# Gated delta rule with HGRN2 in one block: two of a chunk's five preparation tiles are allocated in other PSUM banks

## The chip, the cores and the metric

One core of one Trainium2 chip runs the whole program. The metric is device microseconds of one execution; the median of three runs counts. Beside it there is one execution taken by the hardware profiler, and every line of a profile in this document is of such an execution.

## The reference

The reference is one layer of a diffusion backbone. Its input is 2048 latent tokens (a raster, 64 wide) and 256 context tokens, 1024 features each. All tokens go through a layer norm with a modulation and one wide projection `u @ w_in` in float32. Its columns feed two branches of four heads of 128: branch A is a gated delta rule, branch B an HGRN2 recurrence. Both run forwards and backwards, first over the context, then over the latent tokens. The outputs of both branches are normed, gated, projected, merged by sigmoid gates, projected once more and added to the input.

The change lies in branch A. Cut to what matters (a chunk here has 64 tokens, the kernel uses 128):

```python
decay = where(incl, exp(G_i - G_j), 0)              # G: running sum of log a
a_mat = where(strict, (kb @ k.T) * decay, 0)        # kb = k * beta
w, u  = solve(a_mat + I, [kb * exp(G), v * beta])   # unit lower triangular
attn  = (q @ k.T) * decay
# one step of the scan over chunks, S is 128x128 a head
v_new = u - w @ S
o     = (q * exp(G)) @ S + attn @ v_new
S     = S * exp(G_last) + (k * exp(G_last - G)).T @ v_new
```

`q` and `k` have unit norm per token and head, so the sums of their squares are wanted per token.

## The kernel before, in words

The work comes in this order of the source: modulated inputs `u` (split into a high and a low part, `uhi`, `ulo`, so that three matmuls make one float32 product); the projections of branch A with their convolution, written to DRAM as `qkvD` with features on partitions; branch B; then branch A's preparation, solve and levels; the gate projections; branch A's scan; at last the output stage, which reads both branches and the gates from DRAM.

**Preparation (`prep`, lines 761 to 835).** The 2304 tokens are 18 chunks of 128, two of context and sixteen latent. For each chunk `prep` loads `l` (keys, queries, values of four heads, one SBUF buffer, line 766), and makes up to five PSUM tiles of one bank each on TensorE:

- `pt`, shown as `pk` in the profile (line 773): keys transposed to tokens on partitions. ScalarE sums their squares (777) and copies them to `kv` (778).
- `pq` (780, latent chunks only): queries transposed. ScalarE sums their squares (784), and nothing else reads it.
- `pv` (791): values transposed. VectorE scales them into `kv` (794), which is stored to `knvD`.
- `pkk` (812): keys times keys, straight from `l`. VectorE multiplies it with the decay and the step sizes into `an`, eight instructions (817).
- `pkq` (820, latent only): keys times queries, also from `l`. VectorE multiplies it with the decay, two instructions (824), and the result is stored to `atN` (825).

The decay comes from a scan on VectorE (806), an exponential on ScalarE (808) and a mask on GpSimd (810); it depends on none of the five. All five tiles have the tag `t` in the pool `pc`, with `bufs=3`: a slot is given to the next tile when the last reader of its former tile is through.

**Solve and levels (837 to 903).** Groups of four chunks go through `solve` on VectorE (850, 852: 31 elimination steps on 32x32 blocks), then `levels` joins the blocks with small matmuls in `lvt`, one bank. Preparation of one group, levels of the group before and the solve stand in this order in the source (906 to 928).

**Gate projections (`gate_block`, 224 to 233).** 24 blocks of 128 columns, in groups of 512 tokens; a group is 24 matmuls (217 to 219) into a bank of the pool `pj2`, which has two, a copy out on VectorE (232, even groups) or ScalarE (230, odd) and a store to `gT`. Their weights come through one buffer `ws`: load (202), ScalarE (203), GpSimd (204). After the preparation's code stand twenty blocks on token groups 0 and 1 (938 to 939); their groups 2 and 3 are spread over the scan (`late_block`).

**Scan (`stepA`, 959 to 1008).** Eighteen steps, each with one chunk forwards and one backwards. A step's products (`mm4`, 974) go to tiles `psA` in the pool `pd`, two banks with the tag `A`; from step 9 on two in three of them go to four further banks, `pd2`, which are those of `pc`. The scan's SBUF pool takes the place of `u` of groups 0 and 1, so the scan begins once the gate blocks have read these.

The eight PSUM banks while `prep` runs: two of `pj2`, two of `pd`, three of `t`, one of `lv`.

What sets the order: the source is traced once, and a scheduler then orders each engine's instructions at build time, by the order of the source and a simulated timeline (`schedule_with_timeline_sim=True`). It gives out PSUM slots and writes the waits. On the chip each engine and each DMA queue runs its instructions in that fixed order.

Of the kernel before, what the change touches and what calls it, by code (L numbers as in the profile page):

```python
# [8 lines left out]
F32 = mybir.dt.float32  # L9
# [7 lines left out]
P = 128  # L17
# [7 lines left out]
H = 4  # L25
# [14 lines left out]
def block_kernel(ctx, tc, x, c, ctx_in, c_ctx, w_mod, b_mod, w_in, conv_w, a_log, dt_bias,  # L40
# [699 lines left out]
    pd = pdx.enter_context(tc.tile_pool(name="pd", reuse_waits="tile", bufs=2, space=PSUM))  # L740
# [4 lines left out]
    with tc.tile_pool(name="rc", reuse_waits="tile", bufs=2, side="right") as rc, \  # L745
# [15 lines left out]
        def prep(pos):  # L761
# [15 lines left out]
                ac.activation(out=junk, in_=pt[:, h, :], func=AF.Square, accum_out=sk[:, h:h + 1])  # L777
            ac.copy(out=kv[:, 0], in_=pt)
            if lat:
                pq = pc.tile([P, H, P], F32, tag="t", name="pq", bufs=3)  # L780
                for h in range(H):
                    te.transpose(pq[:, h, :], qT[:, h, :], ident)
                for h in range(H):
                    ac.activation(out=junk, in_=pq[:, h, :], func=AF.Square, accum_out=sq[:, ch, h:h + 1])
# [3 lines left out]
            ve.scalar_tensor_tensor(out=nbz[:, :, ch, :], in0=beta[:, :, ch, :], scalar=-1.0,  # L788
                                    in1=sk.unsqueeze(1).to_broadcast([P, 2, H]), op0=ALU.mult, op1=ALU.mult)
            ve.tensor_tensor(out=nbze[:, :, ch, :], in0=nbz[:, :, ch, :], in1=erem[:, :, ch, :], op=ALU.mult)  # L790
            pv = pc.tile([P, H, P], F32, tag="t", name="pv", bufs=3)
            for h in range(H):
                te.transpose(pv[:, h, :], vT[:, h, :], ident)
            ve.tensor_tensor(out=kv[:, 1], in0=pv, in1=nk.unsqueeze(2).to_broadcast([P, H, P]), op=ALU.mult)
# [111 lines left out]
        for i in range(len(grp) + 2):  # L906
            pl = list(range(grp[i][0], sum(grp[i]))) if i < len(grp) else []
            ll = list(range(grp[i - LAG][0], sum(grp[i - LAG]))) if 0 <= i - LAG < len(grp) else []
            if IL == 0:
                for ch in pl:  # L910
                    prep(ch)
                for ch in ll:
                    levels(ch)
            elif IL == 3:
                for ch in ll:
                    levels(ch)
                for ch in pl:
                    prep(ch)
            else:
                while pl or ll:  # L920
                    if pl:
                        prep(pl.pop(0))
                    if ll:
                        levels(ll.pop(0))
                        if IL == 2 and ll:
                            levels(ll.pop(0))
            if 0 <= i - LAG + 1 < len(grp):
                solve(*grp[i - LAG + 1])
# [20 lines left out]
    if True:  # L949
        SA = []  # L950
        for d in range(2):
            t = rd.tile([P, H, P], F32, tag=f"S{d}", name=f"S{d}")
# [291 lines left out]
```

## Time and profile before

| | us |
|---|---|
| median of 3 runs | 2232.41 (2229.06 to 2242.11) |
| the profiled execution | 2233.26 |
| its span, first to last instruction | 2231.6 |
| busy: TensorE, weight loads, VectorE, ScalarE, GpSimd | 2114.9, 1767.6, 1404.9, 925.3, 688.2 |
| mean granted TensorE clock | 0.985 of full speed |

PE is TensorE, PEld its weight loads, DVE VectorE, ACT ScalarE, POOL GpSimd, SPq the queue of DMAs. Matmuls overlap in the pipeline, so the duration of one (388 ns at 512 columns) is longer than its share of the engine's time. A wait is listed as "engine line waited for: us in total, times, longest"; a line of a timeline gives start, duration, engine, line, tiles, number of instructions and in brackets the idle time before it with what ended it.

### The profile page before, as it was taken

The page shows a single profiled execution, that of the slowest core. Times are in us where ns is not written, and L with a number is a line of the kernel's source. Part 1 is how long each engine was busy: PE and PEld are TensorE (multiplying, and loading weights), DVE is VectorE, ACT ScalarE, POOL GpSimd, SP SyncE. Part 2 cuts the span into 40 slices and gives each one's busy share as a digit, 9 for nine tenths or more (in the row PEclk, how much of TensorE's full clock was granted, in tenths as well). Part 3 has the DMA queues.
Part 4 walks back from the last instruction along what each step waited for, and adds up shares of the span by engine and source line. Part 5 has one row for each costly group of instructions (what it writes and reads, how often), then busy time and mean ns, then how long its engine had stood idle before and what let it go on. Part 6 is the DMA issues. An engine that isn't in the chain of part 4 may idle for free. (4 is left out here: it accounts for less than half of the span.)

```text
span 2231.6 us, 40198 instructions
## 1 busy us (share of the span) xinstructions
PE 2114.9 (95%) x15056; PEld 1767.6 (79%) x15056; DVE 1404.9 (63%) x3225; ACT 925.3 (41%) x2334; POOL 688.2 (31%) x672
## 2 busy tenths in 40 slices
PE   8999999999999999999998988999989888999998
PEld 3778888888888888888776776788778877888887
DVE  4826666727776777786588788733332348766665
ACT  4623222224443444443455554344453354444441
POOL 3413433412222323234333332221133224433331
PEclk9999999999999999999999999999999999999999
DMA  9312222223323433336777778776888864444432
GB/s 340 110 35 76 64 71 77 83 76 95 106 87 100 126 95 104 101 104 195 219 224 225 255 241 214 228 231 208 236 276 278 258 228 147 145 136 127 142 95 80
DMA packets 308277, 348.15 MB, mean 156 GB/s; under 512 B 78635, under 2 KB 218161, under 8 KB 308083
## 3 DMA queue, kind: packets, MB, share of 16 engines
q1 hardware_dynamic: 306067, 338.26, 49.1%
q0 software_dynamic: 2016, 7.34, 0.9%
q8 instruction: 118, 1.93, 0.4%
q14 instruction: 76, 0.62, 0.1%
HBM read 230.46 MB, written 115.06 MB: 155 GB/s over the span
## 5 line engine op out<-in xcount | busy, mean ns | idle before, releaser
L217 PE MATMUL ps<-uhi,wh 128*128 128x512 f32 (+1 forms) x1824 | 708.2, 388 | 2.9 <-DVE uhi L306 2.6
L218 PE MATMUL ps<-ulo,wh 128*128 128x512 f32 (+1 forms) x1824 | 707.6, 388 | 3.4 <-POOL ulo L311 1.7
L219 PE MATMUL ps<-uhi,wl 128*128 128x512 f32 (+1 forms) x1824 | 705.3, 387 | 0.0
L218 PEld LDWEIGHTS ps<-ulo,wh 128*128 128x128 f32 x1824 | 345.9, 190 | 66.7 <-POOL ulo L311 2.8
L217 PEld LDWEIGHTS ps<-uhi,wh 128*128 128x128 f32 x1824 | 345.7, 190 | 66.4 <-DVE uhi L306 3.9
L219 PEld LDWEIGHTS ps<-uhi,wl 128*128 128x128 f32 x1824 | 345.6, 189 | 62.1 <-POOL wl L204 0.4
L204 POOL TENSOR_TENSOR wl<-ws,wh 128x512 fp32r<-128x512 f32 x144 | 200.2, 1391 | 551.7 <-ACT wh L203 494.4
L203 ACT CAST wh<-ws 128x512 fp32r<-128x512 f32 x144 | 89.4, 621 | 309.5 <-DMA ws<-in_w_in_dram 213.9
L419 DVE SCALAR_TENSOR_TENSOR acc<-raw,cols,acc 128x512 f32<-128x512 f32 x192 | 152.8, 848 | 0.9
L1143 PE MATMUL py<-yh,wab 128*128 128x256 f32 x512 | 145.9, 286 | 5.8 <-DVE mg L1146 5.4
L1144 PE MATMUL py<-yl,wab 128*128 128x256 f32 x512 | 145.1, 284 | 1.3 <-POOL yl L1126 1.3
L1145 PE MATMUL py<-yh,wab 128*128 128x256 f32 x512 | 144.6, 283 | 0.0
L1162 PE MATMUL pso<-uhi,mh 128*128 128x512 f32 x256 | 102.6, 402 | 7.8 <-ACT mh L1148 4.7
L605 POOL TENSOR_TENSOR bg<-s,fz 128x512 f32<-128x512 f32 (+1 forms) x36 | 37.8, 1049 | 224.9 <-ACT X L585 86.7
L1143 PEld LDWEIGHTS py<-yh,wab 128*128 128x128 f32 x512 | 97.7, 191 | 8.0 <-DVE mg L1146 6.6
L1164 PE MATMUL pso<-uhi,ml 128*128 128x512 f32 x256 | 102.2, 399 | 0.6 <-DVE ml L1149 0.6
L1163 PE MATMUL pso<-ulo,mh 128*128 128x512 f32 x256 | 101.8, 398 | 0.0
L1144 PEld LDWEIGHTS py<-yl,wab 128*128 128x128 f32 x512 | 97.7, 191 | 2.1 <-POOL yl L1126 1.7
L1145 PEld LDWEIGHTS py<-yh,wab 128*128 128x128 f32 x512 | 98.7, 193 | 0.2
L1126 POOL TENSOR_TENSOR yl<-gt,yh 128x512 fp32r<-128x512 f32 x32 | 45.0, 1408 | 148.3 <-ACT yh L1125 148.3
L998 DVE SCALAR_TENSOR_TENSOR S<-S,gl,psA 128x128 f32<-128x128 f32 x136 | 38.3, 342 | 82.5 <-PE psA L979 82.4
L1136 ACT ACTIVATE mg<-mg 128x512 f32<-128x512 f32 x64 | 40.4, 632 | 113.0 <-DMA mg<-gT 110.4
(374 smaller groups left out, 3942.3 us busy)
## 6 DMA issues: line engine op xcount, KB each, us to landing
ws<-in_w_in_dram SPq DMA_DIRECT2D x144, 256.0 KB, 3.4
gT<-gt SPq DMA_DIRECT2D x96, 256.0 KB, 3.6
kv<-knvD SPq DMA_DIRECT2D x36, 512.0 KB, 5.1
kq<-qkvD SPq DMA_DIRECT2D x32, 512.0 KB, 6.0
an<-atN SPq DMA_DIRECT2D x32, 512.0 KB, 6.2
mg<-gT SPq DMA_DIRECT2D x64, 256.0 KB, 3.4
qkvD<-acc SPq DMA_DIRECT2D x48, 256.0 KB, 2.3
l<-qkvD SPq DMA_DIRECT2D x16, 768.0 KB, 6.5
```

Of the source, the lines that this page charges most:

```text
L203: ac.copy(out=wh[:, j:j + 4, :], in_=ws)
L204: po.tensor_tensor(out=wl[:, j:j + 4, :], in0=ws, in1=wh[:, j:j + 4, :].bitcast(F32), op=ALU.subtract)
L217: te.matmul(out=ps, lhsT=wh[:, k, :], rhs=uhi[gi][:, k, :], start=(k == 0), stop=False)
L218: te.matmul(out=ps, lhsT=wh[:, k, :], rhs=ulo[gi][:, k, :], start=False, stop=False)
L219: te.matmul(out=ps, lhsT=wl[:, k, :], rhs=uhi[gi][:, k, :], start=False, stop=(k == KB - 1))
L419: ve.scalar_tensor_tensor(out=a_, in0=raw[:, o + k:o + k + n], scalar=wk, in1=a_, op0=ALU.mult, op1=ALU.add)
L1143: te.matmul(out=py[:, i, :], lhsT=wh[:, k, ms_], rhs=yh[i][:, k, :], start=(k == 0), stop=False)
L1144: te.matmul(out=py[:, i, :], lhsT=wh[:, k, ms_], rhs=yl[i][:, k, :], start=False, stop=False)
L1145: te.matmul(out=py[:, i, :], lhsT=wl[:, k, ms_], rhs=yh[i][:, k, :], start=False, stop=(k == H - 1))
L1162: te.matmul(out=ps, lhsT=mh[:, k, ts_], rhs=wout[0][k][:, ns], start=(k == 0), stop=False)
L1163: te.matmul(out=ps, lhsT=mh[:, k, ts_], rhs=wout[1][k][:, ns], start=False, stop=False)
L1164: te.matmul(out=ps, lhsT=ml[:, k, ts_], rhs=wout[0][k][:, ns], start=False, stop=(k == KB - 1))
```

## The change

`pq` and `pv` are allocated in the pool `pd` with the tag `A` (two banks, the scan's `psA`) instead of `pc` with the tag `t`. `pk`, `pkk` and `pkq` stay in the three slots of `t`.

```diff
--- before.py
+++ after.py
@@ -777,7 +777,7 @@
                 ac.activation(out=junk, in_=pt[:, h, :], func=AF.Square, accum_out=sk[:, h:h + 1])
             ac.copy(out=kv[:, 0], in_=pt)
             if lat:
-                pq = pc.tile([P, H, P], F32, tag="t", name="pq", bufs=3)
+                pq = pd.tile([P, H, P], F32, tag="A", name="pq")
                 for h in range(H):
                     te.transpose(pq[:, h, :], qT[:, h, :], ident)
                 for h in range(H):
@@ -788,7 +788,7 @@
             ve.scalar_tensor_tensor(out=nbz[:, :, ch, :], in0=beta[:, :, ch, :], scalar=-1.0,
                                     in1=sk.unsqueeze(1).to_broadcast([P, 2, H]), op0=ALU.mult, op1=ALU.mult)
             ve.tensor_tensor(out=nbze[:, :, ch, :], in0=nbz[:, :, ch, :], in1=erem[:, :, ch, :], op=ALU.mult)
-            pv = pc.tile([P, H, P], F32, tag="t", name="pv", bufs=3)
+            pv = pd.tile([P, H, P], F32, tag="A", name="pv")
             for h in range(H):
                 te.transpose(pv[:, h, :], vT[:, h, :], ident)
             ve.tensor_tensor(out=kv[:, 1], in0=pv, in1=nk.unsqueeze(2).to_broadcast([P, H, P]), op=ALU.mult)
```

## The prediction

> **What bounds the kernel now.** I read the head of the page first (busy time of each engine), then the engines' busy time in four stretches: before the delta rule's preparation, the preparation, the scan, the output stage.
>
> ```profile
> PE 2114.9 (95%) x15056; PEld 1767.6 (79%) x15056; DVE 1404.9 (63%) x3225; ACT 925.3 (41%) x2334; POOL 688.2 (31%) x672
> ```
>
> Columns of the next view: stretch, its length, busy time and instruction count of PE, PEld, DVE, ACT, POOL, granted clock, DMA share, GB/s.
>
> ```profile
> 0.00:1036.00 1036.00, 1011.89 (x6905) 821.35 (x6906) 693.07 (x1563) 392.05 (x686) 330.35 (x332) 0.99 0.34 105
> 1036.00:1364.00 328.00, 294.86 (x2107) 241.00 (x2106) 257.89 (x676) 172.52 (x586) 113.99 (x130) 0.98 0.77 236
> 1364.00:1800.00 436.00, 403.30 (x3528) 346.50 (x3528) 179.61 (x538) 185.93 (x589) 100.47 (x114) 0.98 0.78 240
> 1800.00:2232.00 432.00, 404.80 (x2521) 358.77 (x2519) 274.32 (x451) 174.84 (x473) 143.44 (x97) 0.98 0.42 133
> ```
>
> TensorE is the bound of the whole; another engine matters only where it makes TensorE wait. In the preparation (second row, 328 us) TensorE is busy 294.86 us and idle 33.1 us; DVE, with 257.89 us, comes next. What the 33.1 us wait for is in the list of TensorE's waits over the same stretch (waiter, releaser, total us, times, longest):
>
> ```profile
> PE pkk L814 <- ACT kv L778: 9.2, 9, 1.5
> PE pkq L822 <- ACT junk L784: 8.0, 9, 2.8
> PE pkq L822 <- DVE kv L794: 6.1, 5, 1.7
> PE pk L775 <- DMA l<-qkvD: 5.5, 4, 1.9
> ...
> PE pv L793 <- DVE dec L824: 0.5, 1, 0.5
> ```
>
> The first three rows are what the change touches. `pkk` and `pkq` multiply tiles that already lie in SBUF (`kT`, `qT`), so the squares and copies named as releasers (L778, L784, L794) give them no data; they free a PSUM slot. Five tiles of a chunk share a ring of three: `pkk` gets the slot of `pk`, and `pkq` that of `pq` or `pv`. The three rows add up to 23.3 us. One chunk in the timeline (start, duration) shows why the slot is late:
>
> ```profile
> 1115.14 0.60 PE L775 MATMUL pk<-ident,l 128*128 128x128 f32 x4
> ...
> 1119.20 0.63 ACT L808 ACTIVATE dec<-dec 128x512 f32<-128x512 f32 x1 [2.75 <-DVE dec L806]
> ...
> 1121.16 0.26 ACT L777 ACTIVATE junk<-pk 128x128 bf16<-128x128 f32 x1
> ...
> 1123.24 1.16 PE L814 MATMUL pkk<-l 128*128 128x128 f32 x8 [0.91 <-ACT kv L778]
> ...
> 1124.71 1.16 PE L822 MATMUL pkq<-l 128*128 128x128 f32 x8 [0.31 <-ACT junk L784]
> ...
> 1127.04 0.52 SPq L766 DMA_DIRECT2D l<-qkvD  x1
> ```
>
> `pk` is in PSUM at about 1115.7, but ACT squares it only at 1121.16, behind the exponential of the decay (L808), which had itself waited for DVE. TensorE fills the 8.1 us between `pk` and `pkk` with gate matmuls, comes to `pkk` before ACT is through, and stands. The next load of `l` goes out only at 1127.04, after `pkq`, the last reader of its single buffer.
>
> The waits also cost clock. The granted clock is the third number from the end in these rows; the row after them is the `pkq` inside the first one:
>
> ```profile
> 1220.00:1230.00 10.00, 7.14 (x34) 5.92 (x36) 9.62 (x36) 6.39 (x24) 3.69 (x6) 0.83 0.69 182
> 1260.00:1270.00 10.00, 9.34 (x71) 7.70 (x72) 8.58 (x30) 6.34 (x22) 2.28 (x2) 0.83 0.89 316
> 1300.00:1310.00 10.00, 8.23 (x44) 6.63 (x45) 9.48 (x31) 5.29 (x20) 3.64 (x3) 0.66 0.69 233
> ```
>
> ```profile
> 1224.01 2.08 PE L822 MATMUL pkq<-l 128*128 128x128 f32 x8 [1.88 <-ACT junk L784]
> ```
>
> The eight `pkq` matmuls took 2.08 us there, against 1.16 us in the chunk above. Of 10 us each, 0.17 + 0.17 + 0.34 of full speed is missing: 6.8 us of work.
>
> **The change, part by part.** No instruction, DMA or byte is added or removed. The 16 `pq` and 18 `pv` tiles (four transposes each) go to two other banks; nothing moves past another instruction in the source. The banks are the scan's:
>
> ```profile
> L979 PE MATMUL psA<-S,kq x544: 270/275/426, 1362.4 to 1793.7; 128*128 128x128 f32 x182
> ```
>
> Its first matmul starts at 1362.4, when the preparation is over, so the two banks lie idle until then and their new tenants delay nothing. If the last chunk's `pv` holds a bank when the scan is ready, the scan loses at most its DVE read, under 1 us. I take 0.
>
> *Removed.* With `pk`, `pkk` and `pkq` alone in a ring of three, no tile waits for another of its own chunk: 23.3 us go, and the 0.5 us of `pv` behind L824 too; 23.8 us.
>
> *Added.* The next chunk's `pkk` and `pkq` now take slots that this chunk's DVE reads free (L817, L824). All five groups can follow each other at once, so the reload of `l` can go out some 9 us earlier, and TensorE can run up to a chunk ahead until it meets those reads. The order on each queue is fixed when the kernel is built, from modelled durations; where the chain of preparation runs later on the chip than in that plan, TensorE stands at the next slot. That it does run late shows in a wait of DVE's:
>
> ```profile
> DVE dec L806 <- DMA atN<-dec: 22.6, 10, 5.7
> ```
>
> The decay tile waits for its own store, 22.6 us in ten scans; that stays. Bounds of the new wait: 0.5 us (the `pv` row, the only one in which a tile waits for the previous chunk's DVE read) and 23.8 us (the same lateness, met at another slot). I take 9.2 us, the `pkk` row, as the nearest: about one wait of 1 us in every second of the 18 chunks, at the first of the two tiles that meet the limit, the second then following it. Behind a waiting `pkk` stand `pkq` and the gate matmuls, so it is lost in full, as now. Less than 0.5 us is excluded unless other waits shrink too (the rival on the chain); more than 23.8 us takes another mechanism (the rival on DVE). `pk` waiting for `l`, 5.5 us, may fall with the earlier issue or rise with a closer plan: 0 to twice that, so I leave it as it is.
>
> *Clock.* Of these waits 14.6 of 23.8 us go; in proportion the clock gives 6.8 x 14.6 / 23.8 = 4.2 us, between 0 and 6.8.
>
> The Trainium skill ("TensorE: Matmul & The Clock Gate", section "HAM oscillation — how this bites in real kernels") warns of idle gaps above about 3.4 us as what drops the clock. The trace differs: a stretch with clock 0.83 follows a wait of 1.88 us. By the rule the clock term would be 0 and the sum 4.2 us less.
>
> *Does the gain reach the end?* While the scan runs, gate matmuls share its queue. The scan's matmuls (first fence) and the gate's (second) in the same two stretches:
>
> ```profile
> 1700.00:1725.00 25.00, 9.57 (x80) 1.00 0.84 264
> 1775.00:1800.00 25.00, 18.89 (x149) 0.96 0.82 275
> ```
>
> ```profile
> 1700.00:1725.00 25.00, 17.05 (x72) 1.00 0.84 264
> 1775.00:1800.00 25.00, 2.09 (x9) 0.96 0.82 275
> ```
>
> Beside 72 gate matmuls in 25 us the scan gets 80 of its own through; beside 9 it gets 149. So fill slows the scan, not its own chain alone, and fill done earlier lets the scan end earlier. The output stage follows. I carry the gain over in full; the least is 0 (first rival).
>
> *Sum.* 14.6 + 4.2 = 18.8 us off. The profiled execution took 2233.26 us (span 2231.6, 1.7 around it): 2233.3 - 18.8 = 2214.5. The median of the runs is 0.85 us lower, so 2214 us.
>
> **Rivals.**
>
> *The waits only move (no change).* 18 chunks in 328 us are 18.2 us each, on a chain of decay scan, exponential, squares, products and store. If that chain is about 1.3 us a chunk longer than planned, TensorE loses it at some slot, L817's if not L778's; then the 23.8 us come back, and the clock with them: 2233 less a few us, about 2230. For it: the store waits, untouched and as large as the sum. Against it: a chunk's squares can now run ahead of the exponential that held them up, which shortens the chain. That the scan's banks are not free would end here too; the 1362.4 speaks against it.
>
> The Trainium skill (same page and section) tells of a matmul kernel in which double-buffering PSUM gave no further gain. It speaks for this rival; here three rows of waits name the slot, so I leave its chance as the rows give it.
>
> *DVE takes over (slower).* Chunks packed closer put their DVE work in a row ahead of the gate's copies (L232), which free the projection's two banks.
>
> ```profile
> L806 DVE TENSOR_TENSOR_SCAN dec<-gb,after 128x512 f32<-128x512 f32 x36 | 47.6, 1324 | 37.9 <-DMA atN<-dec 22.6 <-issue 9.4 <-DMA gb<-gD 5.1
> ...
> L817 DVE SCALAR_TENSOR_TENSOR an<-pkk,nbz,dec 128x128 f32<-128x128 f32 x137 | 37.8, 342 | 0.2
> L824 DVE TENSOR_TENSOR dec<-pkq,dec 128x512 f32<-128x512 f32 x30 | 20.6, 686 | 1.8 <-PE pkq L822 1.4
> ...
> L232 DVE COPY gt<-ps 128x512 f32<-128x512 f32 x19 | 13.0, 682 | 0.6 <-PE ps L219 0.5
> ```
>
> ```profile
> PEld ps L217 <- DVE gt L232: 0.3, 1, 0.3
> ```
>
> A chunk's burst is 2 x 1.32 + 8 x 0.342 + 2 x 0.686 = 6.8 us. A group of 24 gate matmuls takes 24 x 17.05 / 72 = 5.7 us, so a copy (0.68 us) may be 5.0 us late before TensorE stands. Behind a whole burst each of 19 copies costs 1.8 us, 34 us: 2214.5 + 34 = about 2248. It decides from 18.8 / 19 = 1 us a copy, a lateness of 6 us. For it: DVE's 257.89 of 328 us. Against it: 0.3 us of such waits now, and copies spread through the burst.
>
> *The chain itself gets shorter (more gain).* With squares and products early, all of the 33.1 us and 6.8 us of clock could go: 2233.3 - 39.9 = 2193.
>
> **How the numbers follow.** The forecast has 0.48: 2214, its own range 2203 (new waits 0.5 us, clock in full) to 2222. No change 0.29, about 2230; slower, about 2248, 0.14; more gain, about 2193, 0.09. From these: faster 0.57, same 0.29, slower 0.14, with 0.5% of 2232, 11 us, as what a measurement of this kernel can tell. The range takes in the no-change case with some us above and nearly all of the larger gain: 2195 to 2238; the slower rival is left out.
>
> **What the profile afterwards would show.** Right: TensorE's waits of `pkk` and `pkq` on L778, L784, L794 gone; the five groups of a chunk in one run; fewer stretches below clock 1.00 between 1036 and 1364; the scan's first matmul some 19 us before 1362.4; the scan's first bank with no wait on L794. Wrong: waits of `pkk` or `pkq` on L817 or L824 near 20 us (first rival), waits of the gate's matmuls on L232 (DVE), or a scan that starts earlier and ends at 1793 as now, the freed time then idle in the third stretch.

## The result: slower by one per cent, and the profile after

The changed kernel takes 2257.57 us (median of 6 runs, 2253.49 to 2261.01), the kernel before, run beside it, 2235.89 us (6 runs): a ratio of 1.0101 [1.0082, 1.0120]. The profiled execution took 2258.08 us, its span is 2256.4 us, 24.8 us more than before.

First the head of the page of the changed kernel:

```profile
PE 2123.3 (94%) x15056; PEld 1774.9 (79%) x15056; DVE 1411.1 (63%) x3225; ACT 926.5 (41%) x2334; POOL 683.8 (30%) x672
```

TensorE runs the same 15056 matmuls. It is idle for 2256.4 - 2123.3 = 133.1 us, against 2231.6 - 2114.9 = 116.7 us before: 16.4 us. The other 8.4 us are busy time, for the same work at a lower clock: 0.980 against 0.985. Now the stretches, cut at the scan's first and last matmul (columns as in the prediction):

```profile
0.00:1036.00 1036.00, 1011.71 (x6902) 820.69 (x6903) 691.44 (x1562) 392.47 (x686) 324.85 (x332) 0.99 0.34 105
1036.00:1382.70 346.70, 301.01 (x2082) 246.36 (x2080) 286.19 (x730) 177.37 (x596) 114.14 (x131) 0.96 0.75 225
1382.70:1822.40 439.70, 404.74 (x3546) 348.50 (x3547) 157.98 (x482) 181.61 (x579) 100.42 (x114) 0.96 0.76 236
1822.40:2256.40 434.00, 405.82 (x2530) 359.36 (x2529) 275.50 (x452) 175.03 (x476) 144.38 (x98) 0.98 0.42 134
```

The same two middle stretches of the kernel before, with the scan's own cuts:

```profile
1036.00:1362.40 326.40, 293.26 (x2067) 239.56 (x2066) 256.33 (x673) 172.52 (x586) 113.27 (x130) 0.98 0.77 236
1362.40:1797.90 435.50, 402.80 (x3560) 346.19 (x3559) 181.13 (x541) 185.19 (x587) 101.18 (x115) 0.98 0.78 240
```

The stretch before the scan is 20.3 us longer, the scan 4.2 us, the rest is unchanged. Before the scan TensorE is idle for 346.70 - 301.01 = 45.7 us, against 33.1: 12.6 us. And (1 - clock) times the length is about 13.9 us, against 6.5: 7.4 us (the clock here has two digits; stretches of 10 us give 13.7 and 6.8). The two give 20.0 of the 20.3 us.

Yet the preparation itself became faster. Key transposes (`pk`, L775), first of the kernel before, then of the changed one (count, duration min/median/max, first and last start):

```profile
L775 PE MATMUL pk<-ident,l x72: 270/272/330, 1038.6 to 1352.6; 128*128 128x128 f32 x72
```

```profile
L775 PE MATMUL pk<-ident,l x72: 270/273/447, 1039.2 to 1294.6; 128*128 128x128 f32 x72
```

The last chunk's keys are transposed 58 us earlier. What TensorE waits for instead, between 1030 and 1400 us of the changed kernel:

```profile
PE pk L775 <- DMA l<-qkvD: 17.7, 9, 3.6
PE ps L217 <- DVE gt L232: 6.8, 4, 3.3
PE lvt L888 <- DVE N L885: 4.5, 4, 3.1
PE pkq L822 <- DVE dec L824: 4.3, 5, 1.4
PE psA L979 <- POOL wl L204: 2.9, 1, 2.9
PE lvt L900 <- DVE yt L897: 2.5, 2, 2.1
PE lvt L876 <- ACT Nb L902: 1.9, 1, 1.9
```

No row names L778, L784 or L794 any more: the 23.8 us are gone. Taken by tile, up to the scan's first matmul, these waits replace them (before in brackets): `pk` 19.0 (5.5), the levels' `lvt` 11.4 (3.7), the gates' `ps` 7.9 (0), `pkq` 4.3, the scan's first `psA` 2.9 (0). That is 13.5 + 7.7 + 7.9 + 4.3 + 2.9 = 36.3 us more for 23.8 us less, 12.5 us net, which is the idle time found above.

The timeline of one chunk of the changed kernel shows where the largest comes from:

```profile
1101.91 0.63 PE L775 MATMUL pk<-ident,l 128*128 128x128 f32 x4 [0.72 <-DMA l<-qkvD]
...
1103.24 1.06 PE L814 MATMUL pkk<-l 128*128 128x128 f32 x8
...
1104.14 1.06 PE L822 MATMUL pkq<-l 128*128 128x128 f32 x8
...
1105.29 1.22 DVE L806 TENSOR_TENSOR_SCAN dec<-gb,after 128x512 f32<-128x512 f32 x1
1106.54 2.79 SPq L802 DMA_DIRECT2D gb<-gD  x2
...
1109.42 0.38 SPq L766 DMA_DIRECT2D l<-qkvD  x1
...
1115.23 0.63 PE L775 MATMUL pk<-ident,l 128*128 128x128 f32 x4 [2.09 <-DMA l<-qkvD]
```

The five groups follow each other without a gap. `l` is free when `pkq` ends at 1105.20. But its reload goes out at 1109.42, because the two loads of the gate rows (`gb`, L802) stand ahead of it in SP's queue, and they wait for the decay scan on VectorE that reads their buffers (L806). `l` lands about 5.8 us after its issue, and TensorE stands for 2.09 us. Of the 15 reloads that follow a `pkq`, the middle one goes out 4.2 us after it in the changed kernel and 1.2 us before the change. And with some 18 us a chunk, a delay was then mostly hidden: 5.5 us of waits in all.

### The profile page after: what moved, and what is told of

Its sections match the earlier page's. It is cut to its first block, busy times and chain, and to the rows that moved or that the text cites. A ratio compares the mean times of both kernels' runs of the same rounds, so it can differ in the third digit from the quotient of the medians.

```text
span 2256.4 us, 40213 instructions
## 1 busy us (share of the span) xinstructions
PE 2123.3 (94%) x15056; PEld 1774.9 (79%) x15056; DVE 1411.1 (63%) x3225; ACT 926.5 (41%) x2334; POOL 683.8 (30%) x672
## 5 line engine op out<-in xcount | busy, mean ns | idle before, releaser
L422 POOL TENSOR_TENSOR acc<-acc,sg 128x512 f32<-128x512 f32 (+1 forms) x56 | 71.6, 1296 | 47.8 <-ACT sg L421 47.8
```

## The experiments

Two theories were tested. *Queue:* with packed chunks the reload of `l`, late in SP's queue, takes the place of the ring, and the gates' copies behind VectorE (L232) add to it. *Levels:* VectorE does more of the preparation early, its first solve comes later, and the levels and the scan with it. A third reason stood beside both: an edit can make the scheduler order thousands of instructions anew, and the new order may be worse by itself. In the recorded expectations this third reason is called scatter; packing is the general form of *Queue*, conservation says that TensorE makes up the same lateness at some other wait, and the waits theory is that TensorE's waits set the time, not the start of the levels. Ratios are to the kernel before, run beside each.

### The two tiles one at a time

```diff
 # e2_pq_only, e18_pq_again: pq in pd, pv as before
-            pv = pd.tile([P, H, P], F32, tag="A", name="pv")
+            pv = pc.tile([P, H, P], F32, tag="t", name="pv", bufs=3)
 # e3_pv_only: pv in pd, pq as before
-                pq = pd.tile([P, H, P], F32, tag="A", name="pq")
+                pq = pc.tile([P, H, P], F32, tag="t", name="pq", bufs=3)
```

> Only pq goes to the scan's banks; pv stays in the ring with pk, pkk and pkq. One tile per chunk (pkq) then still waits for a slot of its own chunk (pk, freed by ACT L778). Packing theory: period between 13.5 and 18 us, time between before and after, ratio 1.000 to 1.010. Conservation theory: about 1.000 to 1.005, the waits at pkq on L778. Scatter theory: no order between this run, the next and the full change.

> Only pv goes to the scan's banks; pq stays in the ring. As with pq alone, pkq waits for pk's slot. Packing theory: as with pq alone, ratio 1.000 to 1.010, period the same within 1 us. Conservation theory: 1.000 to 1.005. Scatter theory: may lie over 0.7% away from pq alone.

> The kernel before with `pq` alone in the scan's banks, the same kernel as in e2_pq_only, timed in five rounds to narrow its ratio. If that version is truly faster: ratio 0.994 to 0.998, waits of `pkq` on `kv` near 11 us again, since the order is fixed when the kernel is built. Rival (its 0.4% was the chip's day): ratio 0.998 to 1.002.

`pq` alone: 0.9959 [0.9940, 0.9977], and in the second series 2225.88 us, 0.9974 [0.9957, 0.9991]. `pv` alone: 0.9978 [0.9964, 0.9992]. Each half is faster than the kernel before, the whole is slower. Neither packing nor conservation had this: both put the halves at 1.000 or above. TensorE's waits of `pq` alone (second series) before the scan:

```profile
PE pkq L822 <- ACT kv L778: 9.8, 9, 2.2
PE ps L217 <- ACT gt L230: 5.7, 1, 5.7
PE pk L775 <- DMA l<-qkvD: 5.4, 4, 2.8
```

Four tiles in three slots keep a ring wait of about 10 us, and `l` stays at its old 5.4 us. The stretch before the scan is still 9.9 us longer than before (336.3 us); the gain of 19.7 us lies in the scan (415.8 us):

```profile
1036.00:1372.30 336.30, 298.83 (x2145) 244.24 (x2144) 277.88 (x731) 175.54 (x595) 106.99 (x125) 0.95 0.77 234
1372.30:1788.10 415.80, 393.84 (x3464) 338.35 (x3463) 160.41 (x480) 181.61 (x576) 103.12 (x116) 0.99 0.78 246
```

VectorE has 160 us of work left in the scan instead of 181, and TensorE is idle there for 22.0 us instead of 32.7. That less VectorE work makes the scan shorter is not shown: the changed kernel has only 158 us of it left there, and its scan is the longer one. So neither stretch may be read alone; their sum counts: 761.9 us before, 752.1 here, 786.4 in the changed kernel.

### The reload of the keys, queries and values

Three edits of the changed kernel aim at `l`: hold each load of `l` until the previous chunk's `kv` has been stored (slower pace); put the loads of `gb` on GpSimd's queue; or split `l` into three tiles with a load each.

```diff
 # e1_pace
+            with tc.issue_after(kvs[0]) if kvs[0] is not None else ExitStack():
...
-            sy.dma_start(out=knvD[ch], in_=kv)
+            kvs[0] = sy.dma_start(out=knvD[ch], in_=kv).ins
 # e9_gb_pool
-                sy.dma_start(out=gb, in_=gD[d, ch].rearrange("h t -> (h t)").partition_broadcast(P))
+                po.dma_start(out=gb, in_=gD[d, ch].rearrange("h t -> (h t)").partition_broadcast(P))
 # e10_l_split
+            lt = [rc.tile([P, H, P], F32, tag=f"l{j}", name=f"l{j}", bufs=1) for j in range(3)]
+            for j in ((0, 1, 2) if lat else (0, 2)):
+                sy.dma_start(out=lt[j], in_=qkvD[ch, :, j])
```

> The changed kernel, with the load of the next chunk's l put behind the store of this chunk's kv in the SP queue, about where it went out before the change. Two banks as changed. Packing theory (the chunks follow each other too closely: TensorE then stands at the reload of l, 17.7 us, behind gate copies, 9.2 us, and at the levels, 11.3 us): the period goes back to about 18 us, the ring's waits stay away, so faster than before by up to 1% (ratio 0.990 to 1.000). Conservation theory (TensorE makes up the preparation chain's lateness at whichever slot or buffer comes next): about 24 us of waits come back at pk on l, ratio 1.000 to 1.005. Scatter theory (any new order of instructions moves the time by a per cent): ratio anywhere from 0.99 to 1.015, with waits in other places.

> The changed kernel, with the loads of gb (the decay's input) issued by GpSimd's queue instead of SP's. In the changed kernel the reload of l goes out 4 to 6 us after pkq, its last reader, because two gb loads that wait for VectorE stand ahead of it in SP's queue (before: 0.3 to 3 us); TensorE then waits 17.7 us for l. Queue theory: l goes out within 2 us, the waits of pk on l fall below 8 us, and the time falls by 10 us or more against the changed kernel, ratio to before 1.000 to 1.006. Landing theory (the loads land later than planned because the DMA engines are busier): waits of pk on l stay at 15 us or more. Scatter theory: time does not follow the waits on l.

> The changed kernel with l as three tiles and three loads of 256 KB (keys, queries, values), each freed by its own last reader; the order in SP's queue is the planner's. pk needs only the keys, which land in about 3.5 us instead of 6.9. Both queue and landing theory: waits of pk on l below 8 us, time down by about 10 us against the changed kernel, ratio to before 1.000 to 1.006. If the waits at the gate's copies and the levels count for as much, the time stays above 1.006.

Measured: 1.0011 [0.9992, 1.0029], 1.0003 [0.9986, 1.0020] and 1.0030 [1.0015, 1.0045]; `pk` waits 11.4, 7.3 and 9.9 us in all. Each gives back 0.7 to 1.0 of the 1.0%. The split stays above its expected 8 us; its loads of 256 KB land after 4.4 us (median), not 3.5. With `gb` on GpSimd's queue TensorE waits before the scan for:

```profile
PE ps L217 <- DVE gt L232: 9.3, 3, 3.1
PE pk L775 <- DMA l<-qkvD: 7.3, 6, 3.1
PE pkq L822 <- DVE dec L824: 5.5, 7, 2.0
PE pkk L814 <- DVE an L817: 5.5, 4, 1.7
```

The wait on `l` falls from 17.7 to 7.3 us, those on the gates' copies and on the ring's DVE reads rise: idle time before the scan goes from 45.7 to 38.7 us only. The Trainium skill ("DMA: Bandwidth & Descriptors", section "Issuing engines are not separate DMA queues") says that issuing from several engines only saves the issuing time, usually small beside the transfer. Here it was not the issue itself that took time: in the chunk above the `l` load stood 4 us behind a load that waited. With `gb` elsewhere the middle reload goes out 1.2 us after `pkq`.

If the queue matters only for packed chunks, the same edit must give nothing elsewhere. It was made in the kernel before and in the one with `pq` alone:

> The kernel before with the one line of the gate rows' load (`gb`, L802) on GpSimd's queue; none of the two tiles moved. Theory (the loads of `gb` hold up the reload of `l` only where the preparation is packed as in the kernel after): before, `pk` waits for `l` only 5.5 us and the ring of three waits 23.8 us, so the edit finds little to give back; ratio 0.997 to 1.003, ring waits 18 to 26 us, `pk` 3 to 7 us. Rival (moving `gb` is worth about 1% in any kernel, and the change has no part in it): ratio 0.988 to 0.993. Second rival (any edit that replans moves the time by up to 0.5% either way): outside 0.997 to 1.003 with no wait that accounts for it.

> Only pq in the scan's banks, gb loads on GpSimd's queue. Queue theory: little to win, since pk waits only 4 us for l there: ratio 0.993 to 0.997, as pq alone within its interval. Scatter theory: may lie 0.7% away from pq alone.

In the kernel before it costs 0.4%: 1.0039 [1.0022, 1.0056]; there `pk` waits for `l` 3.6 us and the ring waits, with `pv`, are 17.7 us. With `pq` alone: 1.0044 [1.0026, 1.0062], against 0.9959 and 0.9974 without the edit, so 0.7 to 0.9% worse. Only the fully changed kernel gains, by 1.0%. So the edit has no general merit. But both controls lie outside what the queue theory had expected (0.997 to 1.003 and 0.993 to 0.997), where the third reason had put them, so they do not show that the changed kernel gained by the queue and not by a new order. In the control no single wait accounts for the loss: TensorE is idle for 110.2 us in all, 6.5 us less than before, and its clock is 0.981 against 0.985. Its profiled execution, 2235.16 us, is also the fastest of its ten (median 2242.01), so the trace shows little of the 0.4%.

### The gates' copies

```diff
 # e11_gate_copies_act; e13_gb_pool_copies_act has the gb edit as well
-            if g % 2:
+            if g % 2 or (g == 0 and i >= 24 - NLATE):
                 ac.copy(out=as_rows(t), in_=col_to_row(ps))
```

> The changed kernel, with the copies of group 0 of the twenty late gate blocks on ScalarE (all of their copies before the scan then are). DVE theory: the waits of the gate's matmuls on L232 (6.8 us) go and VectorE is freed of about 14 us in the stretch, so the levels' waits on VectorE (7 us of 11.4) shrink: down by 8 to 15 us against the changed kernel, ratio to before 1.003 to 1.007. If ScalarE is as late as VectorE, the waits turn up on L230 and the ratio stays at 1.010.

> The changed kernel with gb loads on GpSimd's queue and the gate's early copies on ScalarE, two edits which alone gave 1.000 and 1.002 where the change alone gave 1.010. If the losses are sums of waits: gains add, ratio 0.990 to 0.995. If the order chosen decides (scatter): ratio 0.997 to 1.006, no better than one of them.

With the late blocks' copies of group 0 on ScalarE: 1.0021 [1.0008, 1.0034]; the waits of `ps` fall from 7.9 to 3.9 us, but `pk`, too, from 19.0 to 12.3, and `lvt` rises to 16.9. Both edits together: 1.0010 [0.9993, 1.0027], no better than the `gb` edit alone, with `lvt` at 21.4 us. The repairs don't add: what one wait gives up, the next takes.

### The first solve and the start of the levels

Two edits move the first solve forward: VectorE may not start the second group's preparation before `fin`, the last step of the first solve (`e5`), or the first group has two chunks instead of four (`e6` the changed kernel, `e7` the kernel before, `e8` `pq` alone).

```diff
 # e5_hold
+                with tc.issue_after(fin) if i == 1 else ExitStack():
                     for ch in pl:
                         prep(ch)
 # e6, e7, e8
-        grp = [(c0, min(CG, NC - c0)) for c0 in range(0, NC, CG)]
+        grp = [(0, NC % CG)] + [(c0, CG) for c0 in range(NC % CG, NC, CG)]
```

> The changed kernel, with VectorE's instructions of the second group's preparation (chunks 4 to 7) queued behind the last step of the first solve. Levels theory: the first solve takes 79 us in the changed kernel (51 before) because the closer packed preparation comes between its steps on VectorE; so levels start later and the chain solve, levels, scan ends later. Freed of that, the first solve takes about 30 us, the first level's store comes near 1175 instead of 1214, and the end moves by most of it: 2220 to 2235 us, ratio to the changed kernel 0.985. Waits theory (TensorE's 45.7 us idle before the scan set the time): the preparation is held up, TensorE waits as much or more, 2250 us or above.

> The changed kernel with groups of 2, 4, 4, 4, 4 chunks instead of 4, 4, 4, 4, 2; the same five solves, the same work. Levels theory: the first solve can begin after two chunks, near 1065 instead of 1089; the first level's store comes 30 to 60 us earlier than 1214 and the end 20 to 45 us earlier: 2212 to 2237 us. Waits theory: no change beyond 0.5%, 2247 to 2268 us.

> The kernel before the change with groups of 2, 4, 4, 4, 4. Levels theory: the first level's store 30 to 50 us ahead of 1198, the end 15 to 40 us earlier, ratio 0.982 to 0.993. Waits theory: ratio 1.000 within 0.4%, since no wait of the ring goes.

> Only pq in the scan's banks, groups of 2, 4, 4, 4, 4. Levels theory: both gains add, ratio to before 0.978 to 0.990, the fastest of all. Waits theory: as pq alone, 0.996.

1.0063 [1.0048, 1.0078], 1.0045 [1.0028, 1.0063], 1.0088 [1.0073, 1.0103] and 1.0093 [1.0077, 1.0110]. `e5` and `e6`, 2245.4 and 2242.7 us, fall between what the levels theory and the waits theory expected; `e7` and `e8` miss both. The levels' first matmuls (L876; count, durations, first and last start) in the kernel before and in `e7`:

```profile
L876 PE MATMUL lvt<-n,an x576: 185/191/213, 1163.5 to 1619.0; 32*32 32x32 f32 x192
```

```profile
L876 PE MATMUL lvt<-n,an x576: 184/191/238, 1129.4 to 1619.7; 32*32 32x32 f32 x192
```

The levels start 34 us earlier, end 0.7 us later, and the kernel is slower. In the changed kernel they start 42 us (`e5`) and 27 us (`e6`) earlier, and the gain is 0.4 and 0.6%, no more than other edits of it give. So an earlier start of the levels does not explain the time by itself, and the levels theory fell. Nor does the wait on `l`: it is longer in `e6` than in the changed kernel,

```profile
PE pk L775 <- DMA l<-qkvD: 21.5, 11, 4.1
```

and about the same in `e5`, 21.4 us, and yet both are faster than the changed kernel.

### The order itself

Four edits that change no dependence, only where a tile's matmuls stand in the source: `pv`'s transposes ahead of the small VectorE operations, or `pkk` ahead of the decay, in both kernels.

```diff
 # e4_pv_early (before), e14_after_pv_early
+            pv = pd.tile([P, H, P], F32, tag="A", name="pv")      # e4: pc, tag "t", bufs=3
+            for h in range(H):
+                te.transpose(pv[:, h, :], vT[:, h, :], ident)
             ve.tensor_scalar(out=sk, in0=sk, scalar1=EPS, scalar2=None, op0=ALU.add)
 # e16_before_pkk_early, e15_after_pkk_early: pkk and its four matmuls right behind the store of kv
```

> The kernel before the change, with pv's allocation and transposes written in the source ahead of the five small instructions on the squares (L785 to L790). No resource changes. Packing and conservation theories: ratio 1.000, within 0.3%, waits of pkk and pkq in the ring about 23 us as before. Scatter theory: the time moves by 0.5% or more.

> The changed kernel with pv's allocation and transposes ahead of the five small instructions in the source, the neutral edit that left the kernel before at 0.9995. Waits theory: ratio to before 1.008 to 1.012, as the change. Scatter theory: 1.000 to 1.006 is as likely, with the scan's stretch back at 422 to 427 us from 439.7.

> The changed kernel with pkk's allocation and its four matmuls ahead of the decay in the source; they depend on l alone, so no resource changes. Waits theory: 1.008 to 1.012. Scatter theory: anywhere from 0.998 to 1.012.

> The kernel before the change with the same move of pkk. Waits theory: 1.000 within 0.3%, the ring's waits at about 23 us. Scatter theory: 0.993 to 1.010.

Before: 0.9995 [0.9981, 1.0010] and 0.9990 [0.9974, 1.0006]. Changed: 1.0110 [1.0073, 1.0147] and 1.0104 [1.0069, 1.0138], with `pk` at 18.0 and 21.1 us. The one per cent stands against these edits. They are hardly a test, though: in the traces at most 27 of the 15056 places in TensorE's order of matmuls hold another matmul, while the change itself alters 4403 of them and the `gb` edit 3839. So they show that this one order loses 1.0% each time, not that another order of the changed source would.

### Kernels side by side

Idle and clock loss ((1 - clock) times span) are TensorE's, of the one profiled execution; the ratio is that of the timed runs.

| kernel | ratio | span | idle | clock loss | span less both |
|---|---|---|---|---|---|
| before | 1 | 2231.6 | 116.7 | 33.5 | 2081.4 |
| changed | 1.0101 | 2256.4 | 133.1 | 45.1 | 2078.2 |
| e2, `pq` alone | 0.9959 | 2217.0 | 109.8 | 28.8 | 2078.4 |
| e18, the same | 0.9974 | 2222.7 | 113.5 | 28.9 | 2080.3 |
| e3, `pv` alone | 0.9978 | 2227.5 | 114.6 | 35.6 | 2077.3 |
| e9, changed + `gb` queue | 1.0003 | 2230.7 | 112.5 | 37.9 | 2080.3 |
| e13, e9 + copies | 1.0010 | 2232.7 | 114.7 | 40.2 | 2077.8 |
| e11, changed + copies | 1.0021 | 2236.6 | 119.5 | 33.5 | 2083.6 |
| e10, changed + `l` split | 1.0030 | 2241.5 | 121.0 | 40.3 | 2080.2 |
| e17, before + `gb` queue | 1.0039 | 2233.4 | 110.2 | 42.4 | 2080.8 |
| e7, before + small first group | 1.0088 | 2247.4 | 125.7 | 36.0 | 2085.7 |
| e15, changed + `pkk` early | 1.0104 | 2258.5 | 126.1 | 51.9 | 2080.5 |

TensorE's own work is 2077 to 2086 us in all of these, and 2072 to 2079 us in the eight kernels that the table leaves out; what differs is the time that it stands and the clock that it loses.

## Why the prediction was wrong, step by step

- **TensorE is the bound.** Right, as the last column shows.
- **Removed, 23.8 us.** Right: the three rows are gone, the five groups run in one piece, and the preparation ends 58 us earlier. The store wait of `dec`, which was to stay at 22.6 us, fell to 5.2 us.
- **Added, 9.2 us at L817 and L824, and `pk` "as it is".** This is the step that failed. The new slot waits were small (4.3 us, all on L824), but the other ends of the same chain were not priced. The waits of `pk` went from 5.5 to 19.0 us, 17.7 of them on `l`, outside their bounds of 0 to 11; the gates' `ps` waits 7.9 us instead of none and the levels' `lvt` 11.4 instead of 3.7. With the `psA` wait, 36.3 us were added where 9.2 were priced. The text saw that "the reload of `l` can go out some 9 us earlier" and looked neither at what stands ahead of it in SP's queue nor at the 5.8 us that it takes to land. `e9` shows the queue's part in the wait: with `gb` out of the way `pk` waits 7.3 us. What that part is worth in time is not shown (below).
- **DVE takes over (rival).** Right in kind, too high in size: 6.8 us of waits on L232, not 34.
- **The levels (no term).** `lvt` rose by 7.7 us, and 7.9 of its 11.4 us are waits on VectorE (2.3 of 3.7 before). That they stand behind VectorE's preparation work, which now falls closer together, is a reading, not tested.
- **Clock, 4.2 us gained.** Wrong in sign. Shorter ring waits did not bring clock; the new waits are longer and cost more. By 10-us stretches between 1036 and the scan, the loss went from 6.8 to 13.7 us.
- **Does the gain reach the end.** Not tested as meant, since the scan started 20 us later. In `pq` alone it went the other way round: the scan started 10 us later, and ended 10 us earlier.
- **The sum.** 23.8 us out and 36.3 us in before the scan, 7.4 us of clock on top, 4.2 us in the scan: 24.1 of the 24.8 us, where 18.8 us of gain were forecast. The rival "the waits only move" had the right mechanism, but put it at one slot and let it give back no more than it took.

What stays open. In the scan the changed kernel waits in more places than the one with the `gb` edit. First the changed kernel's largest waits there, then those of `e9`:

```profile
PE psA L979 <- ACT vx L985: 13.1, 10, 4.7
PE psA L979 <- DVE r L991: 7.3, 5, 2.2
PE psA L979 <- ACT o L985: 4.7, 2, 2.7
PE psA L979 <- DMA an<-atN: 2.9, 2, 2.1
```

```profile
PE psA L979 <- ACT vx L985: 5.3, 7, 1.1
PE psA L979 <- DMA an<-atN: 4.4, 4, 3.5
PE psA L979 <- ACT o L985: 3.4, 3, 2.0
PE psA L979 <- DVE r L991: 1.3, 1, 1.3
```

No `l` is loaded in the scan and its source is the same, so the order that the scheduler chose is the likely reason for these 12.5 us of idle time (35.0 against 22.5). The two stretches of `e9`:

```profile
1036.00:1373.70 337.70, 299.04 (x2073) 242.07 (x2071) 292.17 (x730) 174.81 (x592) 129.65 (x163) 0.97 0.77 230
1373.70:1798.10 424.40, 401.88 (x3553) 345.21 (x3553) 160.60 (x483) 184.12 (x582) 101.91 (x115) 0.97 0.78 245
```

Of the 25.7 us by which its span is shorter than the changed kernel's, 9.0 lie before the scan and 15.3 in it. The other edits agree: the scan takes 439.7 to 443.3 us in the changed kernel and its near copies `e14` and `e15`, and 416.9 to 427.3 us in the seven edits that changed the order. No run here separates that order from the queue; every edit that made the scheduler order the changed kernel anew (`e1`, `e5`, `e6`, `e9`, `e10`, `e11`, `e13`) gave back 0.4 to 1.0%, whatever it aimed at. So where TensorE waits instead is shown; how much of the one per cent is the queue's and how much this one order's stays open. No run gives `l` a second buffer, which would test the queue most directly.

## What to carry to other kernels

When a ring of buffers is what paces a loop, ask before lifting it what paces the loop next: for a buffer with one slot, follow its reload to the queue that issues it and read what stands ahead of it there and what that waits for. Lift one limit at a time and time each half; here each tile alone gained 0.2 to 0.4%, and both together lost 1.0%. And where a scheduler orders the whole program, a control that makes the same edit in the kernel without the change is worth more than a further edit: here it showed that moving `gb` is not worth 1% in general. An edit of the changed kernel that leaves the suspect alone is the other control: that `e5` and `e6` gave back 0.4 and 0.6% with `l` waited for as long as ever shows that a gain after an edit need not come from what the edit aimed at.

## What the runs showed of the hardware

A wait can cost TensorE twice its own length. In the changed kernel a matmul of the levels waited 3.14 us in the middle of a chunk, and what followed ran slower:

```profile
1295.61 0.39 PE L814 MATMUL pkk<-l 128*128 128x128 f32 x2
1299.14 0.65 PE L888 MATMUL lvt<-n,yt 32*32 32x32 f32 x32 [3.14 <-DVE N L885]
...
1301.16 1.91 PE L822 MATMUL pkq<-l 128*128 128x128 f32 x8
1302.72 0.77 PE L217 MATMUL ps<-uhi,wh 128*128 128x512 f32 x1
...
1304.58 0.63 PE L218 MATMUL ps<-ulo,wh 128*128 128x512 f32 x1
...
1305.53 0.39 PE L218 MATMUL ps<-ulo,wh 128*128 128x512 f32 x1
```

The eight `pkq` matmuls took 1.91 us instead of 1.06, a gate matmul 0.63 instead of 0.39, until about 1305. The granted clock of these 10-us stretches:

```profile
1290.00:1300.00 10.00, 6.72 (x66) 5.44 (x65) 9.72 (x28) 3.47 (x10) 1.60 (x2) 0.91 0.94 299
1300.00:1310.00 10.00, 10.00 (x54) 8.43 (x54) 9.69 (x21) 6.84 (x28) 5.05 (x8) 0.74 0.49 108
```

0.9 + 2.6 = 3.5 us of full speed are lost, on top of the wait of 3.14 us. Over the whole span the loss comes in drops of about 1.7 or 3.4 us (stretches of 0.83 and 0.66); some 20 drops lie in the changed kernel and 15 in the one before, nearly all with idle time in the same stretch or the one ahead. Not every wait brings one: the 2.09 us of `pk` in the chunk above were followed by the full clock, the 1.88 us of `pkq` in the kernel before by a drop. The Trainium skill ("TensorE: Matmul & The Clock Gate", section "A second HAM failure mode: psum-queue depth-cycling") tells of short idle times between groups of matmuls that make the clock go up and down; the trace agrees, while the gap of about 3.4 us that the same page gives in the section before it is longer than the one here.
